# Gated linear attention: the decayed queries times the state on quarters of the array, right behind the level products, into two PSUM banks; the next queries' transposes in another bank

## The chip, the cores and the metric

The kernel is one inference step of one layer of a hybrid decoder. It runs on one core of a Trainium2 chip. The metric is device time in microseconds (us) from one launch to its end; of several executions the median is given. The engines of the core are TensorE (PE in the profile; its weight loads are listed apart as PEld), VectorE (DVE), ScalarE (ACT), GpSimd (POOL) and SyncE (SP), which here issues the DMAs. Matmuls read SBUF and write PSUM, whose eight banks hold 512 float32 numbers for each of 128 partitions.

## The reference

The layer has two groups of heads behind one input projection (sliding-window attention and gated linear attention), an output projection, and a squared-ReLU MLP. The change is in the gated linear attention of the 2048 prompt tokens: 4 heads, keys and queries of 64, values of 128. Per head there is a state S of 64 x 128, which starts at zero. Cut to what matters:

```python
b = jnp.cumsum(log_a, axis=2)                      # inside a chunk
attn = einsum('bnthk,bntshk->bnhts', qc, exp(causal(b_t - b_s)) * kc)
o_intra = einsum('bnhts,bnshv->bnthv', attn, vc)
q_dec = qc * exp(b)                                # the decayed queries
def step(S, xs):
    o = einsum('bthk,bhkv->bthv', qd, S)           # decayed queries times the state
    S = ab[..., None] * S + einsum('bthk,bthv->bhkv', kd, vv)
    return S, o
o = o_intra + o_inter                              # then RMSNorm, gate, output projection
```

The outputs are the tokens after the layer, the last 128 keys and values, and the states.

## The kernel before

The kernel goes through the tokens in stages: input projection of the attention columns with windowed attention, input projection of the linear-attention columns (tiles named gproj) with the gated linear attention in between, output projection (out), and the two MLP matrices (u... and dn). The change lies in the second of these, at about 330 to 690 us.

**Chunks.** The 2048 tokens are 16 chunks of 128, index i. `gla(i, ...)` is a generator that does one chunk. At each `yield n` the loop that drives it issues n matmuls of other work on TensorE, the "fill": the projection of later chunks (gproj, 128 x 384 each) and near the end the output projection. The numbers are in `G_FILL = (34, 14, 16, 8, 20)`. TensorE executes in the order in which the calls stand (its wrapper, line 142, chains every instruction to the one before), so this list sets how much other work stands between two steps of a chunk. The order on VectorE and ScalarE is made by a scheduler, within the dependencies; where two instructions must not change places the code says so.

**Steps of a chunk.** (1) `qk_T`: four transposes (tile gqk) bring keys and queries to 128 partitions, which hold two heads of 64. VectorE copies the keys (kt); ScalarE copies the queries to `qz[rows, r]`, r = 0 or 1 for the upper or lower 64 partitions, the other half being zero. (2) After 34 fills the norm and gate of the chunk before are finished (`finish_out`: squares on ScalarE, line 1180, tile og on VectorE, line 1189) and transposed (ogT); then z, the gate of the next chunk, is projected into bank "d". (3) VectorE and ScalarE make the weighted keys and queries of 7 levels (XK, XQ), which treat the triangle of a chunk block by block, and kd, the keys decayed to the chunk's end. (4) The level products: tiles gl and gh in two banks of kind "c", then ds, the new part of the state, in bank "d". The level products and ds have 128 rows and 64 columns of the array each, and write to partitions 0 to 63 and 64 to 127 in turn. (5) VectorE multiplies qz by the decay to get qd, of 128 x 2 x 2 x 128, half of it zero (line 1269). (6) VectorE puts the level products into AH under masks (line 1163), VectorE and ScalarE copy them to AT, the triangle transposed (lines 1273 to 1275, the names `put` and `done`); VectorE then makes the next state (line 1280, which reads ds). (7) After 20 fills, tile o in bank "e": per head first qd times the state So, then AT times the values gv, summed in PSUM; each is a float32 product on the whole array, 128 x 128 by 128 x 128.

The PSUM banks "d" and "e" are there once, "a", "b" and "c" twice; a tile takes over a bank when all readers of the tile before are done. In the profile the two passes of a float32 product are two MATMUL rows, each with a weight load.

Of the kernel before, what the change touches and what calls it, by code (L numbers as in the profile page):

```python
# [16 lines left out]
ALU = mybir.AluOpType  # L17
# [4 lines left out]
P = 128  # L22
# [19 lines left out]
NL = len(LEVELS)  # L42
# [85 lines left out]
def f32(ap):  # L128
    return ap.bitcast(F32)
# [23 lines left out]
def hybrid_step_kernel(ctx: ExitStack, tc: tile.TileContext, I, O):  # L153
    nc = tc.nc
# [18 lines left out]
    te, ac, dv = (InOrder(tc, engine) for engine in (nc.tensor, nc.scalar, nc.vector))  # L173
# [4 lines left out]
    def bank(shape, kind, name):  # L178

        return ps.tile(shape, F32, tag=kind, name=name, bufs=1 if kind in "de" else 2)  # L180
# [240 lines left out]
    half_of = slice(HD), slice(HD, P)  # L421
# [606 lines left out]
    def places(name, shape, n=1, kind=F32):  # L1028
        return cycle([sp.tile(shape, kind, name=f"{name}{u}") for u in range(n)])

    S = [sp.tile([P, 2, P], F32, name=f"S{u}") for u in range(2)]
    glrT = [sp.tile([P, P], F32R, name=f"glrT{u}") for u in range(3)]
    AT = sp.tile([P, 4, P], F32, name="AT")
# [3 lines left out]
    XK = sp.tile([P, NL, 2, P], F32, name="XK")  # L1037
    XQ = sp.tile([P, NL, 2, 2, P // 2], F32, name="XQ")
    sgs, prs = places("sg", [P, 512]), places("pr", [P, 256])
    qds = places("qd", [P, 2, 2, P])  # L1040
    decs = places("dec", [P, NL + 1, 2, P])
    befores, afters = places("before", [P, 2, P]), places("after", [P, 2, P])
    kts = places("kt", [P, 2, P], 2)
    qz = sp.tile([P, 2, 2, P], F32, name="qz")
# [58 lines left out]
    def qk_T(i, gp, n, kind="d"):  # L1103

        pt = bank([P, 2, 2, n], kind, f"gqk_{i}")
        for g in range(2):
            for a in range(2):
                src = gp[:n, (1 - a) * 256 + g * P : (1 - a) * 256 + (g + 1) * P]
                te.transpose(pt[:, g, a, :], src, ident[:n, :n])
        kt, q = (next(kts), qz) if n == P else (s_kt, s_qz)  # L1110
        nc.vector.tensor_copy(kt, pt[:, :, 0, :])
        for r, rr in enumerate(half_of):
            nc.scalar.activation(q[rr, r], pt[rr, :, 1, :], AF.Copy, scale=0.125)
        return kt
# [60 lines left out]
    def finish_out(i, og_src, sg, n, kind):  # L1175

        ssq = sp.tile([P, 4], F32, tag="ossq", name=f"ossq_{i}", bufs=2)
        junk = sp.tile([P, P], mybir.dt.bfloat16, tag="ojunk", name=f"ojunk_{i}", bufs=1)
        for h in range(4):
            nc.scalar.activation(junk[:n], og_src(h), AF.Square, accum_out=ssq[:n, h : h + 1])  # L1180
        rs = sp.tile([P, 4], F32, tag="ors", name=f"ors_{i}", bufs=2)
        rsqrt_mean(sp, rs[:n], ssq[:n], n, P, 4)
        if i == NB:
            yield 44, True
            yield 44, True
        og = next(ogs) if i < NB else gp_s[:, :512].rearrange("p (h d) -> p h d", h=4)
        for h in range(4):
            with tc.issue_after(put[0].ins) if i == NB else nullcontext():
                nc.vector.scalar_tensor_tensor(
                    og[:n, h, :], og_src(h), rs[:n, h : h + 1], sg[:n, h * P : (h + 1) * P],  # L1190
                    op0=ALU.mult, op1=ALU.mult,
                )
        for _ in range(S_WAIT[0] if i == NB else 1):
            yield 44, True
        pt = bank([P, 4, P], kind, f"ogT_{i}")
        for h in range(4):
            te.transpose(pt[:, h, :n], og[:n, h, :], ident[:n, :n])
        if i == NB - 1:
            hi, lo = late_mix
            nc.vector.tensor_copy(hi, pt)  # L1200
            nc.vector.tensor_tensor(lo, pt, f32(hi), op=ALU.subtract)
        else:
            mo = next(mos)
            nc.scalar.activation(mo[:, :, :n], pt[:, :, :n], AF.Copy)
            nc.sync.dma_start(mix_d[i][:, 4:8, :], mo[:, :, :n])

    def decayed(i):

        before, after = next(befores), next(afters)
        yield from decays(i, P, before, "d" if i else "b")  # L1210
        nc.gpsimd.memset(after, 0.0)
        pre[i] = before, after

    def gla(i, gp, og=iter(())):

        assert {(i, 0), (i, 1)} <= projected
        before, after = pre.pop(i)
        next(og, None)  # L1220
        kt = qk_T(i, gp, P)
        dec = next(decs)
        following = decayed(i + 1) if i < NB - 1 else iter(())
        yield G_FILL[0] + 3 * (i == 1) if i else G_FIRST_FILL, True
        deque(og, 0)
        put_diagonal(i, AH, gp, P)
        for l, b in enumerate(LEVELS):
            if l < (4 if i == 2 else NL - 1) or i == 0:
                level_sums(before, after, dec, l, b)
            else:  # L1230
                with tc.issue_after(put[0].ins):
                    level_sums(before, after, dec, l, b)
            if l == NL - 1:
                kd = next(kds)
                pair = i // 2 + 1 if i % 2 == 0 and i < NB - 2 else 0
                turned = keys_decayed(after, kt, next(kdTs), P, "e", kd, pair)
                nc.scalar.activation(dec[:, NL], before, AF.Exp, scale=1.0 / 16)
            weighted(XK, XQ, dec, kt, qz, l, b)
        next(turned)
        deque(following, 0)  # L1240
        yield G_FILL[1] - 3 * (i == 1), True
        assert {(i, c) for c in range(4)} <= projected
        sg = gate(i, gp, P)
        yield G_FILL[2], True
        deque(turned, 0)
        yield G_FILL[3], True
        low = bank([P, 4, 4, P // 4], "c", f"gl_{i}")
        high = bank([P, 512], "c", f"gh_{i}")
        mid = high[:, :256].rearrange("p (l h q) -> p l h q", l=2, h=4)
        far = high[:, 256:384].rearrange("p (r q) -> p r q", r=2)  # L1250
        levels = [*(low[:, l] for l in range(4)), *(mid[:, l] for l in range(2))]
        for l, gm in enumerate(levels):
            for g in range(2):
                keys = XK[:, l, g] if l else kt[:, g]
                for u, uu in enumerate(half_of):
                    te.matmul(
                        gm[uu, 2 * g : 2 * g + 2], keys[:, uu], XQ[:, l, :, g, u * 32 : u * 32 + 32], start=True, stop=True
                    )
        for g in range(2):
            te.matmul(far[half_of[g]], XK[:, NL - 1, g, :HD], XQ[:, NL - 1, :, g], start=True, stop=True)  # L1260
        gv = gp[:, 512:1024]
        ds = bank([P, 2, P], "d", f"ds_{i}")
        for h in range(4):
            te.matmul(
                ds[half_of[h % 2], h // 2], kd[:, h * HD : (h + 1) * HD], gv[:, h * P : (h + 1) * P],
                start=True, stop=True,
            )
        qd = next(qds)
        nc.vector.tensor_tensor(qd, qz, dec[:, NL].unsqueeze(1).to_broadcast([P, 2, 2, P]), op=ALU.mult)
        for l, gm in enumerate(levels):  # L1270
            put_level(AH, gm, msk[:, l], LEVELS[l])
        for g in range(2):
            nc.scalar.activation(AT[:HD, 2 * g : 2 * g + 2, HD:], far[half_of[g]], AF.Copy)
        put[:] = [nc.vector.tensor_copy(AT[half_of[1], :, half_of[1]], AH[half_of[1]])]
        done = nc.scalar.activation(AT[half_of[0], :, half_of[0]], AH[half_of[0]], AF.Copy)
        put.append(done)
        So, Sn = S[i % 2], S[(i + 1) % 2]
        with tc.issue_after(put[0].ins):
            for g in range(2):
                nc.vector.scalar_tensor_tensor(  # L1280
                    Sn[:, g], So[:, g], dec[:, NL, g, P - 1 : P], ds[:, g], op0=ALU.mult, op1=ALU.add
                )
        yield G_FILL[4], True
        o_ = bank([P, 4, P], "e", f"o_{i}")
        for h in range(4):
            if i > 0:
                te.matmul(o_[:, h, :], qd[:, h % 2, h // 2], So[:, h // 2], start=True, stop=False)
            te.matmul(o_[:, h, :], AT[:, h, :], gv[:, h * P : (h + 1) * P], start=i == 0, stop=True)
        with tc.issue_after(done.ins):
            next(wo_parts, None)  # L1290
        ogs_of[i] = og = finish_out(i, lambda h: o_[:, h, :], sg, P, "e")
        if i == NB - 1:
            yield from og
            for g in range(2):
                for r in range(2):
                    nc.sync.dma_start(O["gla_prompt"][0, 0, 2 * g + r], Sn[half_of[r], g])
# [229 lines left out]
    wo, pre, ogs_of, mixes, late_mix, g_mix, put, placing, x1_first = {}, {}, {}, {}, [], [], [], [], []  # L1526
# [887 lines left out]
```

## Time and profile before

| | |
|---|---|
| median of 3 runs | 2162.13 us (2161.69 to 2163.29) |
| the profiled execution | 2162.71 us, its span 2160.9 us |
| TensorE busy | 2149.6 us, 99% of the span |
| VectorE, ScalarE, GpSimd busy | 71%, 57%, 12% |
| mean granted TensorE clock | 0.999 |
| MATMUL rows o<-S,qd in the trace | 120 (15 chunks of 4 products of 2 passes) |

A row of the time line has the start in us, the length in us, engine, line, operation, output tile <- input tiles, the rows and columns of the array (64\*64 means that one quarter of it is used), the shape that is streamed, and the count of instructions merged. Matmuls overlap, so that what one costs is the distance to the next start and not its length. Idle time in brackets says which engine ended it; "issue" is idle time for which the trace has no releaser.

### The profile page before, as it was taken

The numbers are of one execution on the slowest core, as the hardware profiler recorded it, in microseconds if no ns is written. First come the engines' busy times: TensorE is split into PE (matmuls) and PEld (weight loads), VectorE is DVE, ScalarE is ACT, GpSimd is POOL, SyncE is SP. The second block draws the span as 40 slices with busy tenths as digits, with TensorE's granted clock in tenths as the row PEclk, the third lists the DMA queues.
The fourth block names the chain that finished last, engine by engine and source line by source line (L and its number), as shares of the span: only waits on it lengthen the run. The fifth ranks groups of instructions, "written<-read, shape, count | busy, mean of one in ns | idle before, by whom it ended". The sixth has DMA issues, their size and how long they took to land.

```text
span 2160.9 us, 34240 instructions
## 1 busy us (share of the span) xinstructions
PE 2149.6 (99%) x11799; PEld 1864.0 (86%) x11799; DVE 1529.1 (71%) x3203; ACT 1221.6 (57%) x2625; POOL 258.5 (12%) x417
## 2 busy tenths in 40 slices
PE   9999999999999999999999999999999999999998
PEld 9999999999998888888888888888888888888887
DVE  7999868777775766988888545547766666555566
ACT  7999867566664444655555544445454445444454
POOL 4676511111111100000000000000000000000000
PEclk9999999999999999999999999999999999999999
DMA  7444341234338566777785777668544443766685
GB/s 242 154 147 148 99 117 40 71 106 135 136 126 270 199 216 220 245 269 274 256 279 208 269 247 223 208 199 274 183 171 155 157 150 126 257 203 195 195 267 181
DMA packets 241322, 411.54 MB, mean 190 GB/s; under 512 B 24876, under 2 KB 143132, under 8 KB 237036
## 3 DMA queue, kind: packets, MB, share of 16 engines
q1 hardware_dynamic: 240988, 409.08, 57.1%
q8 instruction: 93, 1.52, 0.3%
q14 instruction: 81, 0.66, 0.1%
q10 hardware_dynamic: 160, 0.27, 0.0%
HBM read 265.82 MB, written 143.99 MB: 190 GB/s over the span
## 4 chain that ended last, share of the span: by engine, by line
PE 93%; DVE 2%; ACT 2%; DMA 1%; issue 1%; POOL 0%; SPq 0%; DVEq 0%; POOLq 0%; ACTq 0%
PE dn L142 27%; PE gproj L142 13%; PE uc L142 8%; PE uX L142 8%; PE out L1419 7%; PE proj L142 6%; PE ue L142 4%; PE ud L142 4%; PE ub L142 4%; PE dsam L142 1%; PE sam L142 1%; PE o L142 1%; PE sc L142 1%; PE pT L142 1%; PE av L142 1%; PE out L142 1%
## 5 line engine op out<-in xcount | busy, mean ns | idle before, releaser
L142 PE MATMUL dn<-o1t,o0s 128*128 128x512 f32 x892 | 347.9, 390 | 0.8 <-DVE o1t L229 0.8
L142 PE MATMUL dn<-o0t,o1s 128*128 128x512 f32 x892 | 347.7, 390 | 0.0
L142 PE MATMUL dn<-o0t,o0s 128*128 128x512 f32 x892 | 347.4, 389 | 0.3 <-DVE f L2075 0.3
L229 DVE TENSOR_TENSOR o1s<-rs,o0s 128x512 fp32r<-128x512 f32 x224 | 154.6, 691 | 220.8 <-ACT o0s L228 218.5
L228 ACT ACTIVATE o0s<-rs 128x512 fp32r<-128x512 f32 x224 | 141.1, 631 | 291.9 <-PE dn L142 261.6
L142 PE MATMUL gproj<-wg,gxh 128*128 128x384 f32 x1024 | 273.2, 342 | 0.0
L142 PEld LDWEIGHTS dn<-o1t,o0s 128*128 128x128 f32 x892 | 167.4, 188 | 37.3 <-DVE o1t L229 1.7
L142 PEld LDWEIGHTS dn<-o0t,o0s 128*128 128x128 f32 x892 | 167.5, 188 | 36.8 <-DVE f L2075 0.7
L142 PEld LDWEIGHTS dn<-o0t,o1s 128*128 128x128 f32 x892 | 167.4, 188 | 35.2
L142 ACT ACTIVATE st<-st 128x512 f32<-128x512 f32 x224 | 141.1, 630 | 100.2 <-DVE st L142 95.1
L142 PEld LDWEIGHTS gproj<-wg,gxh 128*128 128x128 f32 x1024 | 184.2, 189 | 3.5 <-issue 3.1
L142 PE MATMUL uc<-H,s 128*128 128x512 f32 x768 | 186.5, 391 | 0.1
L142 PE MATMUL gproj<-wg,gxl 128*128 128x384 f32 x576 | 185.9, 340 | 0.0
L142 PE MATMUL uX<-H,w 128*128 128x512 f32 x768 | 185.2, 390 | 0.0
L142 PEld LDWEIGHTS uX<-H,w 128*128 128x128 f32 x768 | 144.0, 188 | 30.3
L142 PEld LDWEIGHTS uc<-H,s 128*128 128x128 f32 x768 | 143.0, 188 | 30.6 <-ACT st L142 0.3
L1419 PE MATMUL out<-wo,mt 128*128 128x512 f32 x680 | 158.6, 392 | 0.0
L229 DVE TENSOR_TENSOR o1t<-rt,o0t 128x512 fp32r<-128x512 f32 x223 | 152.7, 685 | 5.3 <-ACT o0t L228 3.7
L218 POOL TENSOR_TENSOR frs<-rs_v,half 128x1 f32<-128x1 f32 (+1 forms) x13 | 11.5, 891 | 1198.6 <-DVE rs_v L216 1198.6
L1419 PEld LDWEIGHTS out<-wo,mt 128*128 128x128 f32 x680 | 126.5, 188 | 26.1
L228 ACT ACTIVATE o0t<-rt 128x512 fp32r<-128x512 f32 x223 | 137.7, 618 | 7.5 <-DMA rt<-t_d 4.8
L142 DVE TENSOR_TENSOR st<-st 128x512 f32<-128x512 f32 x160 | 110.7, 692 | 30.1 <-ACT st L142 25.8
(429 smaller groups left out, 4307.2 us busy)
## 6 DMA issues: line engine op xcount, KB each, us to landing
s_d<-st SPq DMA_DIRECT2D x32, 1792.0 KB, 8.9
rs<-s_d SPq DMA_DIRECT2D x224, 256.0 KB, 3.0
raw<-in_w_up SPq DMA_DIRECT2D x64, 512.0 KB, 4.6
rt<-t_d SPq DMA_DIRECT2D x128, 256.0 KB, 3.9
rt<-in_w_down SPq DMA_DIRECT2D x96, 256.0 KB, 2.9
t<-in_w_down SPq DMA_DIRECT2D x64, 256.0 KB, 3.7
t_d<-t SPq DMA_DIRECT2D x32, 512.0 KB, 5.1
h_d<-ht SPq DMA_DIRECT2D x8, 1280.0 KB, 7.6
```

The source lines that it names most:

```text
L142: ins = call(*a, **k)
L218: return nc.gpsimd.tensor_tensor(out, v[:n], e, op=ALU.pow)
L228: nc.scalar.activation(hi, src, AF.Copy)
L229: return vector.tensor_tensor(lo, src, f32(hi), op=ALU.subtract)
L1419: te.matmul(banks[c], x, w[:, c * 512 : (c + 1) * 512], start=k + u == 0, stop=k == KT - 1 and u == len(products) - 1,)
```

## The change

In step 5 the decayed queries are made without the zero half, in two VectorE instructions of 64 partitions x 256 (qd is now 128 x 2 x 128), ahead of the first fill of step 3 to 4 instead of behind the level products.

The products of qd and the state leave step 7. They stand right behind ds in step 4, and instead of 4 products on the whole array there are 8 of 64 rows x 64 columns: r is the half of the rows (one head), u the half of the queries, hence of the output partitions, g the pair of heads. The results of r = 0 go to bank "e", those of r = 1 to the right half of the bank "d" whose left half holds ds. The products of AT and the values stay where they were and add to the two banks; `finish_out` reads both.

The transposes of the next chunk's keys and queries (gqk) go to a bank of kind "c" instead of "d", which is now occupied until og is made.

```diff
-    qds = places("qd", [P, 2, 2, P])
+    qds = places("qd", [P, 2, P])
...
-        kt = qk_T(i, gp, P)
+        kt = qk_T(i, gp, P, "c")
...
         next(turned)
+        qd = next(qds)
+        for r, rr in enumerate(half_of):
+            nc.vector.tensor_tensor(qd[rr], qz[rr, r], dec[rr, NL], op=ALU.mult)
         deque(following, 0)
         yield G_FILL[1] - 3 * (i == 1), True
...
-        ds = bank([P, 2, P], "d", f"ds_{i}")
+        fourth = bank([P, 4, P], "d", f"ds_{i}")
+        ds = fourth[:, :2]
...
-        qd = next(qds)
-        nc.vector.tensor_tensor(qd, qz, dec[:, NL].unsqueeze(1).to_broadcast([P, 2, 2, P]), op=ALU.mult)
+        So, Sn = S[i % 2], S[(i + 1) % 2]
+        o_ = bank([P, 2, P], "e", f"o_{i}"), fourth[:, 2:]
+        for g in range(2):
+            for u, uu in enumerate(half_of):
+                for r, rr in enumerate(half_of):
+                    if i > 0:
+                        te.matmul(
+                            o_[r][uu, g], qd[rr, g, uu], So[rr, g], start=g == 0, stop=False, skip_group_check=True
+                        )
...
-        o_ = bank([P, 4, P], "e", f"o_{i}")
         for h in range(4):
-            if i > 0:
-                te.matmul(o_[:, h, :], qd[:, h % 2, h // 2], So[:, h // 2], start=True, stop=False)
-            te.matmul(o_[:, h, :], AT[:, h, :], gv[:, h * P : (h + 1) * P], start=i == 0, stop=True)
+            te.matmul(
+                o_[h % 2][:, h // 2], AT[:, h, :], gv[:, h * P : (h + 1) * P], start=i == 0, stop=True, skip_group_check=True
+            )
...
-        ogs_of[i] = og = finish_out(i, lambda h: o_[:, h, :], sg, P, "e")
+        ogs_of[i] = og = finish_out(i, lambda h: o_[h % 2][:, h // 2], sg, P, "e")
```

How the instructions stand: TensorE in one even chunk in the middle of the stage, from the level products to the next queries' transposes, before (S is the state, gp the values and keys, the fill gproj is left out).

```order
L142 MATMUL gh_7494<-XQ,XK 64x128 x2
L142 MATMUL ds_7521<-gp_7093,kd_4983 64x128 [waits DVE_49,Activation_49]
L142 MATMUL ds_7521<-gp_7093,kd_4983 64x128 x3
...
L142 MATMUL o_7559<-S_4976,qd_4991 128x128 [waits PE_49,Activation_49]
L142 MATMUL o_7559<-gp_7093,AT 128x128 [waits DVE_49,Activation_49]
L142 MATMUL o_7559<-S_4976,qd_4991 128x128
L142 MATMUL o_7559<-gp_7093,AT 128x128
...
L142 MATMUL gqk_7591<-ident,gp_7361 128x128 [waits DVE_49,PE_49]
```

The same place in the changed kernel; the new products that write to bank "d" are listed under the name ds.

```order
L142 MATMUL gh_7532<-XQ,XK 64x128 x2
L142 MATMUL ds_7559<-gp_7124,kd_4983 64x128 [waits DVE_49,Activation_49]
L142 MATMUL ds_7559<-gp_7124,kd_4983 64x128 x3
L142 MATMUL o_7564<-S_4976,qd_4991 64x128 [waits PE_49,Activation_49]
L142 MATMUL ds_7559<-S_4976,qd_4991 64x128
...
L142 MATMUL o_7564<-gp_7124,AT 128x128 [waits DVE_49,Activation_49]
L142 MATMUL ds_7559<-gp_7124,AT 128x128 [waits DVE_49]
...
L142 MATMUL gqk_7632<-ident,gp_7397 128x128 [waits PE_49]
```

Eight small products now stand directly behind ds, in turns into the two banks; the four of the whole array are gone from between the AT products; the second AT product has a wait for VectorE of its own, and gqk no longer waits for VectorE.

VectorE in one chunk, from the last weighted keys to the next chunk's gate, before:

```order
L1132 TENSOR_TENSOR XQ<-dec_4992,qz 128x256
L1137 TENSOR_TENSOR kdT_5000<-kdT_5000,kt_4995 128x256
L1095 SCALAR_TENSOR_TENSOR sg_4989<-gp_7093,sg_4989 128x512 [waits DVE_49,Activation_49]
L1269 TENSOR_TENSOR qd_4991<-qz,dec_4992 128x512
L1086 SCALAR_TENSOR_TENSOR before_4993<-z_7430,zt_4998 128x256 [waits PE_49,Activation_49]
```

and now:

```order
L1132 TENSOR_TENSOR XQ<-dec_4992,qz 128x256
L1137 TENSOR_TENSOR kdT_5000<-kdT_5000,kt_4996 128x256
L1242 TENSOR_TENSOR qd_4991<-qz,dec_4992 64x256 x2
L1095 SCALAR_TENSOR_TENSOR sg_4989<-gp_6831,sg_4989 128x512 [waits DVE_49,Activation_49]
L1086 SCALAR_TENSOR_TENSOR before_4993<-z_7199,zt_4999 128x256 [waits PE_49,Activation_49]
```

The scheduler had already put qd this early; it moves by one place, ahead of the gate's product, and is two instructions.

More of the change, by code (lines that the diff above doesn't have):

```diff
@@ L1276, in gla @@
         put.append(done)
-        So, Sn = S[i % 2], S[(i + 1) % 2]
         with tc.issue_after(put[0].ins):
```

## The prediction

> **What bounds the kernel now.** I read the page first: which engine is full, and whose chain ended last.
>
> ```profile
> PE 2149.6 (99%) x11799; PEld 1864.0 (86%) x11799; DVE 1529.1 (71%) x3203; ACT 1221.6 (57%) x2625; POOL 258.5 (12%) x417
> PE 93%; DVE 2%; ACT 2%; DMA 1%; issue 1%; POOL 0%; SPq 0%; DVEq 0%; POOLq 0%; ACTq 0%
> ```
>
> TensorE is the bound overall. Whether it is in the stage that changes is read from the busy times by window: the whole stage with what follows, and single chunks, from one chunk's first level product to the next's.
>
> ```profile
> 330.00:690.00 360.00, 359.98 (x2975) 342.37 (x2974) 272.28 (x819) 224.64 (x668) 61.05 (x62) 1.00 0.36 121
> 690.00:1200.00 510.00, 509.93 (x2444) 426.26 (x2443) 392.06 (x612) 267.20 (x466) 19.20 (x33) 1.00 0.73 244
> 539.16:560.75 21.59, 21.59 (x183) 1.00 0.38 135
> 560.75:582.38 21.63, 21.63 (x182) 1.00 0.40 135
> ```
>
> PE is busy in 359.98 of 360 us, VectorE in 272. "Busy" can hide a stretched matmul, so I looked at the waits of the weight loads in that stretch too:
>
> ```profile
> PEld gl L142 <- issue: 4.0, 15, 0.4
> PEld o L142 <- ACT AT L1275: 0.2, 1, 0.2
> ```
>
> Only one wait of the step that changes is there, 0.2 us once; the first row is 15 entries into the level products and returns below. So the stage lasts as long as its matmuls take, and the following stage runs TensorE just as full (509.93 of 510): time saved on TensorE here comes off the end.
>
> **What is removed.** One chunk's o, before:
>
> ```profile
> 544.94 0.38 PE L142 MATMUL o<-S,qd 128*128 128x128 f32 x2
> 545.16 0.39 PE L142 MATMUL o<-gp,AT 128*128 128x128 f32 x2
> 545.38 0.39 PE L142 MATMUL o<-S,qd 128*128 128x128 f32 x2
> ...
> 546.72 0.49 PE L142 MATMUL gqk<-ident,gp 128*128 128x128 f32 x3
> ```
>
> Eight products in 546.72 - 544.94 = 1.78 us, 0.22 each (0.111 per pass). Four go: 0.89 us per chunk, in the 15 chunks that have a state. The four AT products stay.
>
> **What is added.** Eight products, sixteen passes, of 128 columns streamed on quarters of the array. No row has just that, so I take the nearest. First the level products and ds, which use half the columns:
>
> ```profile
> 538.89 0.34 PE L142 MATMUL gproj<-wg,gxh 128*128 128x384 f32 x1
> 539.16 0.45 PE L142 MATMUL gl<-XQ,kt 128*64 128x64 f32 x8
> ...
> 540.83 0.61 PE L142 MATMUL ds<-gp,kd 128*64 128x128 f32 x8
> 541.36 0.45 PE L142 MATMUL gproj<-wg,gxh 128*128 128x384 f32 x1
> 541.64 0.34 PE L142 MATMUL gproj<-wg,gxl 128*128 128x384 f32 x1
> ```
>
> A gproj normally starts 0.17 after the one before (the pair in the next fence); into gl it takes 539.16 - 538.89 = 0.27, so 0.10 is lost on entering; the "issue" row above is these 15 entries as the weight loads see them (4.0 / 15 = 0.27). ds has 8 passes in 0.53; if as much is lost on leaving, 0.43 remain: two passes at a time, 0.11 per pair, the column halves running together. Then the two places that use fewer rows:
>
> ```profile
> 396.34 0.33 PE L142 MATMUL gproj<-wg,gxh 128*128 128x384 f32 x1
> 396.51 0.33 PE L142 MATMUL gproj<-wg,gxl 128*128 128x384 f32 x1
> 396.77 0.65 PE L142 MATMUL sds<-gp_s,s_kx 64*64 64x128 f32 x8
> 397.35 0.62 PE L142 MATMUL gproj<-wg,gxh 128*128 128x384 f32 x2
> ```
>
> ```profile
> 288.01 0.38 PE L142 MATMUL spt<-ident,ss 128*128 128x128 f32 x2
> 288.32 0.44 PE L142 MATMUL ssc<-kc,qs 64*32 64x128 f32 x8
> 288.56 0.31 PE L142 MATMUL ssc<-kns,qs 64*32 64x64 f32 x8
> ```
>
> sds is the shape of the new products, but all of it on one half of the rows: 0.58 us for 8 passes, of which 0.10 is leaving and about 0.04 the first loads: again pairs at 0.11. ssc has four column groups: 8 passes of 128 columns in 0.24 us, that is four at a time, 0.11 per set and 0.02 more for the first. So independent parts of the array do run together here; what no row shows is the two halves of the rows at once. The Trainium skill, "TensorE: Matmul & The Clock Gate", section "Part 3: Packing small matmuls — row/col tiling", has measured speedups for tiles packed in rows and columns at once; no run here shows that yet.
>
> I take four at a time: 4 sets x 0.11 = 0.44, plus 0.03 for the first loads. Between ds (128 rows) and the new products (64 rows) the array changes its division, and I charge the 0.10 of the other entries: spt to ssc shows it too (288.32 - 288.01 = 0.31 for two passes of 0.11, 0.09 over). Leaving costs the same from sds (397.35) as from ds, so nothing is added there. Block: 0.57 us. Low end 0.44 (no drain, ds and the new products alike to the array), high end 0.44 + 0.03 + 0.20 = 0.67 (drain paid as on entering and on leaving). The Trainium skill, "TensorEngine Tiling (Array Packing)", section "Key Properties", has it that a change of tiling mode, not of tile, drains the array; by that 0.57 holds and not 0.44. The entries above agree with it, but between two divided modes no row stands.
>
> Saved per chunk: 0.89 - 0.57 = **0.32**; over 15 chunks 4.8 us (3.3 at 0.67, 6.8 at 0.44).
>
> **Waits.** AT must be ready when TensorE comes to it. The tightest two chunks:
>
> ```profile
> 566.14 0.60 DVE L1280 SCALAR_TENSOR_TENSOR S<-S,dec,ds 128x128 f32<-128x128 f32 x2
> 566.34 0.40 ACT L1275 ACTIVATE AT<-AH 64x256 f32<-64x256 f32 x1
> 566.53 0.38 PE L142 MATMUL o<-S,qd 128*128 128x128 f32 x2
> ```
>
> ```profile
> 625.46 0.45 PE L142 MATMUL gl<-XQ,kt 128*64 128x64 f32 x8
> 631.19 0.40 ACT L1275 ACTIVATE AT<-AH 64x256 f32<-64x256 f32 x1
> 631.24 0.38 PE L142 MATMUL o<-S,qd 128*128 128x128 f32 x2
> 631.65 0.49 PE L142 MATMUL o<-gp,AT 128*128 128x128 f32 x2
> ```
>
> In the second, AT ends at 631.59 and the first AT product starts 0.41 after the first qd product instead of 0.22: 0.19 is lost. In the changed kernel the block stands ahead of the 20 fills, so TensorE gets to AT at 631.24 + 0.57 = 631.81 by the same clock, 0.22 after AT is there: that wait goes, **0.2 us** in all. The new second wait, of the AT product into bank "d" for the state update that reads ds, ends at 566.74 in the first fence; TensorE comes to it at 566.53 + 0.57 + 0.22 = 567.32. Behind both would stand the next chunk's gqk and all fill. The new products themselves wait for bank "e", in even chunks for the copy of glrT:
>
> ```profile
> 518.76 0.27 ACT L1145 ACTIVATE glrT<-kdT 128x128 fp32r<-128x128 f32 x1
> 519.34 0.61 PE L142 MATMUL ds<-gp,kd 128*64 128x128 f32 x8
> ```
>
> It ends 0.3 us before ds starts. Bank "d" is now held until og is made, and z wants it next; but z stands behind ogT, which needs og anyway. gqk in "c" needs a bank whose reader was the masked copy, done before AT. These edits cost nothing, as long as og stays ahead of ogT: 549.93 + 1.13 = 551.06 against 553.07.
>
> ```profile
> 549.93 1.13 DVE L1189 SCALAR_TENSOR_TENSOR og<-o,ors,sg 128x128 f32<-128x128 f32 x4 [0.46 <-POOL ors L218]
> 553.07 0.60 PE L142 MATMUL ogT<-ident,og 128*128 128x128 f32 x4
> 554.12 0.69 DVE L1269 TENSOR_TENSOR qd<-qz,dec 128x512 f32<-128x512 f32 x1
> 556.57 0.42 DVE L1086 SCALAR_TENSOR_TENSOR before<-z,zt 128x256 f32<-128x256 f32 x1 [1.76 <-ACT zt L980]
> ```
>
> **VectorE.** qd was 0.69; now two instructions of 64 x 256. A product of 256 columns of this kind takes 0.42 (the row at 556.57), whatever its partitions, so 0.84 at most, 0.15 more per chunk. VectorE idles 1.76 us right behind it, waiting for ScalarE; that covers it. Without that cover the masked copies would come 0.15 later, still inside the 0.22 of the tightest chunk.
>
> **Sum.** 4.8 + 0.2 = 5.0 us off the profiled execution's 2162.71 us: 2157.7. That execution is 0.6 above the median, so against 2162.13 I predict **2157.1 us**. One thing moves single executions without the change:
>
> ```profile
> 376.70:380.15 3.45, 3.45 (x36) 0.51 0.34 89
> ```
>
> Here the granted clock was 0.51 for one stretch of 3.4 us, behind a stretch of very small products of the sample tokens: some 1.7 us lost. The three runs differ by 1.6. Whether a later run has this stretch I can't tell; it widens the range by about 1 us.
>
> **Rivals.**
>
> *No drain* between ds and the new products: block 0.44, saved 6.8 + 0.2 = 7.0, 2155.1 us. For it: the columns are divided in two before and after, only the rows change. Against: every change of division in the trace costs about 0.10. Chance 0.12.
>
> *Loads in the open or a double drain:* if the weight loads of a quarter can't run under the products of the same rows, each of the four sets waits for its load. The nearest price is the pair of gl passes of 64 columns, which bounds a load of 64 columns: (540.14 - 539.44) / 12 = 0.058.
>
> ```profile
> 539.44 0.87 PE L142 MATMUL gl<-XQ,XK 128*64 128x64 f32 x24
> 540.14 0.86 PE L142 MATMUL gh<-XQ,XK 128*64 128x64 f32 x20
> ```
>
> Three more loads are 0.17, the block 0.74, saved 2.3 + 0.2: 2159.6 us. The Trainium skill, "TensorE: Matmul & The Clock Gate", section "Part 3: Packing small matmuls — row/col tiling", says that loads overlap with running products only if the row group differs, which is this rival. Against it: sds has all its products on one row group, and 0.11 per pair leaves no room for a load of its own. Chance 0.10.
>
> *The halves of the rows don't run together:* eight pairs instead of four sets, 8 x 0.11 + 0.13 = 1.01 us against 0.89 removed. **Slower** by 0.12 x 15 = 1.8, less the 0.2: 2163.7 us. It decides from a set time of 0.19 up (4 x 0.19 + 0.13 = 0.89). For it: no row shows two halves of the rows at once. Against: four column groups run together at the full rate, and the two halves write to different banks. Chance 0.09.
>
> *AT becomes the bound:* in a chunk like the one at 566 TensorE reaches AT at 566.53 + 0.57 = 567.10, 0.36 us after ScalarE and VectorE are done. If their new order delays the masked copies by more than that in most chunks, the next 0.32 takes the gain (2162) and each further 0.1 costs 1.5 us. Against: the order of VectorE around the copies stays. Chance 0.04.
>
> **Chances.** The forecast has 0.65, and its own range is 2156.0 to 2158.6 (a block from 0.52 to 0.62, and the odd half-clock stretch). A difference of 0.2%, 4.3 us, is about what a measurement of this kernel can tell from none: faster means below 2157.8. Of the forecast's 0.65 some 0.48 lies there, with the 0.12 of no drain 0.60. Slower, above 2166.5, has 0.03, from AT as the bound and a second failure. The rest, 0.37, is the same. The range 2154.7 to 2160.0 takes in all but the last two rivals.
>
> **What would show it.** In the trace of after: sixteen rows of 64\*64 behind ds, with about 0.55 to 0.6 us from their first start to the next gproj less 0.10 for leaving; if they take 1.0, the row halves do not run together. The o rows shrink to four products of 0.22. The period of the chunk at 539 falls from 21.59 to about 21.27. No wait of o for VectorE or ScalarE. The prediction is wrong if the rows of 64\*64 come in pairs 0.11 apart, if "issue" in front of them is well over 0.1, or if a stage behind this one turns out to wait for a DMA that did not move.

## The result: 0.15% slower, and the profile after

The median of 21 runs is 2165.21 us (2162.84 to 2167.74); the kernel before, run beside it, has 2161.90 (2159.75 to 2164.71, 21 runs). The ratio is 1.0015, with a 95% interval of 1.0010 to 1.0021: 3.3 us slower, where 5.0 us faster was forecast. On TensorE itself the change did what it was to do. The page of the changed kernel, total busy times and the chain that ended last:

```profile
PE 2147.0 (99%) x11919; PEld 1856.3 (86%) x11919; DVE 1537.2 (71%) x3219; ACT 1220.7 (56%) x2625; POOL 259.6 (12%) x417
PE 88%; DVE 6%; ACT 4%; issue 1%; DMA 1%; POOL 0%; DVEq 0%; ACTq 0%; SPq 0%
```

TensorE is busy for 2.6 us less than before, but VectorE and ScalarE, 2% each of the chain before, now hold 10% of it together. The busy times of the stage, and of one chunk in its middle (columns: span; then PE, PEld, VectorE, ScalarE and GpSimd busy; clock; DMA share; GB/s), show where:

```profile
330.00:690.00 360.00, 353.02 (x3047) 331.50 (x3042) 276.75 (x826) 222.73 (x662) 61.49 (x62) 1.00 0.36 118
537.92:559.90 21.98, 21.51 (x191) 20.60 (x190) 17.58 (x51) 14.46 (x42) 3.91 (x4) 1.00 0.39 133
```

TensorE was busy for 359.98 of these 360 us and now is for 353.02; the next stage, 690 to 1200 us, is as full as it was (510.00 of 510). The waits of the weight loads in the same stretch (engine, what waited, for what: us in all, times, the longest):

```profile
PEld ds L142 <- ACT kd L1143: 9.2, 9, 1.6
PEld o L142 <- issue: 2.5, 14, 0.3
```

The first row is new. In nine chunks ds waits for kd, the copy of the decayed keys on ScalarE, 9.2 us in all. The second is the entering of the new block, 14 times 0.18. Here is that block, in the chunk of the second window above (TensorE's time line):

```profile
540.23 0.66 PE L142 MATMUL ds<-gp,kd 128*64 128x128 f32 x8 [0.47 <-ACT kd L1143]
540.82 0.32 PE L142 MATMUL o<-S,qd 64*64 64x128 f32 x1
540.82 0.32 PE L142 MATMUL ds<-S,qd 64*64 64x128 f32 x1
540.83 0.32 PE L142 MATMUL o<-S,qd 64*64 64x128 f32 x1
540.84 0.32 PE L142 MATMUL ds<-S,qd 64*64 64x128 f32 x1
540.98 0.27 PE L142 MATMUL o<-S,qd 64*64 64x128 f32 x1
...
541.09 0.27 PE L142 MATMUL o<-S,qd 64*64 64x128 f32 x1
...
541.19 0.27 PE L142 MATMUL o<-S,qd 64*64 64x128 f32 x1
...
541.41 0.44 PE L142 MATMUL gproj<-wg,gxh 128*128 128x384 f32 x1
...
544.98 0.38 PE L142 MATMUL o<-gp,AT 128*128 128x128 f32 x2
...
545.87 0.60 PE L142 MATMUL gqk<-ident,gp 128*128 128x128 f32 x4
```

Sixteen passes come in four sets of four, both halves of the rows and of the columns at once: the sets start at 540.82, 540.98, 541.09 and 541.19, and the next gproj at 541.41. That is 0.59 us, of which 0.10 is leaving. The products of AT alone take 545.87 - 544.98 = 0.89. So the saving is there, and more than its size is lost ahead of ds.

**Why kd is late.** VectorE in one chunk of the kernel before, from the copy of the keys kt to qd; its queries' transposes gqk started at 503.64:

```profile
503.64 0.60 PE L142 MATMUL gqk<-ident,gp 128*128 128x128 f32 x4
504.28 0.42 DVE L1111 COPY kt<-gqk 128x256 f32<-128x256 f32 x1 [0.38 <-PE gqk L142]
504.74 0.90 DVE L1130 TENSOR_TENSOR XK<-dec,kt 128x128 f32<-128x128 f32 x4
505.56 0.17 DVE L216 TENSOR_SCALAR rs_v<-ossq 128x4 f32<-128x4 f32 x1
...
506.85 1.13 DVE L1189 SCALAR_TENSOR_TENSOR og<-o,ors,sg 128x128 f32<-128x128 f32 x4 [0.46 <-POOL ors L218]
...
510.11 0.42 DVE L1137 TENSOR_TENSOR kdT<-kdT,kt 128x256 f32<-128x256 f32 x1
510.53 0.69 DVE L1095 SCALAR_TENSOR_TENSOR sg<-gp,sg 128x512 f32<-128x512 f32 x1
511.14 0.68 DVE L1269 TENSOR_TENSOR qd<-qz,dec 128x512 f32<-128x512 f32 x1
```

The same chunk of the changed kernel:

```profile
502.15 0.60 PE L142 MATMUL gqk<-ident,gp 128*128 128x128 f32 x4
502.79 0.42 DVE L1111 COPY kt<-gqk 128x256 f32<-128x256 f32 x1
503.25 0.49 DVE L1130 TENSOR_TENSOR XK<-dec,kt 128x128 f32<-128x128 f32 x2
504.29 0.17 DVE L216 TENSOR_SCALAR rs_v<-ossq 128x4 f32<-128x4 f32 x1 [0.55 <-ACT ojunk L1180]
504.37 0.51 DVE L1130 TENSOR_TENSOR XK<-dec,kt 128x128 f32<-128x128 f32 x2
505.58 0.35 DVE L1189 SCALAR_TENSOR_TENSOR og<-o,ors,sg 128x128 f32<-128x128 f32 x1 [0.70 <-POOL ors L218]
...
509.37 0.42 DVE L1137 TENSOR_TENSOR kdT<-kdT,kt 128x256 f32<-128x256 f32 x1
509.71 0.84 DVE L1242 TENSOR_TENSOR qd<-qz,dec 64x256 f32<-64x256 f32 x2
510.58 0.69 DVE L1095 SCALAR_TENSOR_TENSOR sg<-gp,sg 128x512 f32<-128x512 f32 x1
```

Two things differ on VectorE. First, the norm's small step rs_v and og of the chunk before stand behind two and four of the products XK, where they stood behind four, and then behind one XK and one XQ more (the scheduler put them there; this order appears in ten of the twelve chunks from the fifth on). Neither is ready: VectorE idles 0.55 us for ScalarE's squares and 0.70 for GpSimd, where it had idled 0.46. So kdT ends 509.79 - 502.15 = 7.64 us behind gqk and not 510.53 - 503.64 = 6.89: 0.75 later. Second, qd now stands ahead of the gate's product sg, which starts 0.79 behind the end of kdT (510.58 - 509.79) where it had started right at it: sg ends 9.12 us behind gqk and not 7.58.

ScalarE's last step of the gate (L1096) waits for sg, and steps of zt, made from z of the next chunk, stand behind it: three before, two now, since the first (L977) has changed places with it. Before, and after:

```profile
511.26 0.64 ACT L1096 ACTIVATE sg<-sg 128x512 f32<-128x512 f32 x1 [0.76 <-DVE sg L1095]
512.28 0.38 ACT L977 ACTIVATE zt<-z 128x256 f32<-128x256 f32 x1
513.13 0.42 ACT L980 ACTIVATE zt<-zt 128x256 f32<-128x256 f32 x1
518.50 0.36 ACT L1143 ACTIVATE kd<-kdT 128x256 f32<-128x256 f32 x1
```

```profile
509.62 0.38 ACT L977 ACTIVATE zt<-z 128x256 f32<-128x256 f32 x1
511.31 0.63 ACT L1096 ACTIVATE sg<-sg 128x512 f32<-128x512 f32 x1 [1.31 <-DVE sg L1095]
512.28 0.42 ACT L980 ACTIVATE zt<-zt 128x256 f32<-128x256 f32 x1
517.92 0.37 ACT L1143 ACTIVATE kd<-kdT 128x256 f32<-128x256 f32 x1
```

So zt ends 9.91 us behind gqk before and 10.55 after, 0.64 later, while sg is 1.54 later. sg has a second follower: behind L1096 GpSimd multiplies the gate twice (L1098, L1100), and in the changed kernel the second of these meets the first sums of the levels on VectorE:

```profile
513.46 1.56 POOL L1100 TENSOR_TENSOR sg<-sg,ggla 128x512 f32<-128x512 f32 x1
513.78 1.38 DVE L1157 TENSOR_TENSOR before<-before 128x128 f32<-128x128 f32 x1
```

This sum takes 1.38 us. In the traces of the ten kernels of this document 137 such sums between 400 and 650 us start inside one of GpSimd's two multiplications. Each ends 0.14 to 0.15 us behind it and takes up to 1.39 us; every other such sum takes at most 0.30. VectorE is held there until GpSimd is done. It happens 18 times in each of the four kernels with qd ahead of the gate's product, and 10 or 11 times in each of the six others.

Behind zt VectorE and ScalarE take turns through the levels of the next chunk (before, after, dec), and kd stands in ScalarE's queue behind most of these exponentials. It ends 15.22 us behind gqk before (518.86 - 503.64) and 16.14 after (518.29 - 502.15); ds comes at 519.34 - 503.64 = 15.70 when nothing holds it. kd had half a microsecond to spare in this chunk, 0.23 in the tightest of the stage's middle. And the lateness is passed on: the next gqk stands behind this ds on TensorE, and its kt, og and kdT behind that. The middle chunks (the eight that start between 470 and 630 us) go from one to the next in 22.24 us on average, where it was 21.58 before.

This is a reading of two traces, in which two delays are mixed; the experiments separate them.

### The profile page after: what moved, and what is told of

Its sections match the earlier page's. It is cut to its first block, busy times and chain, and to the rows that moved or that the text cites. A ratio compares the mean times of both kernels' runs of the same rounds, so it can differ in the third digit from the quotient of the medians.

```text
span 2164.4 us, 34502 instructions
## 1 busy us (share of the span) xinstructions
PE 2147.0 (99%) x11919; PEld 1856.3 (86%) x11919; DVE 1537.2 (71%) x3219; ACT 1220.7 (56%) x2625; POOL 259.6 (12%) x417
## 3 DMA queue, kind: packets, MB, share of 16 engines
q8 instruction: 94, 1.54, 0.3%
## 4 chain that ended last, share of the span: by engine, by line
PE 88%; DVE 6%; ACT 4%; issue 1%; DMA 1%; POOL 0%; DVEq 0%; ACTq 0%; SPq 0%
PE dn L142 27%; PE uc L142 8%; PE uX L142 8%; PE out L1428 7%; PE gproj L142 7%; PE proj L142 6%; PE ud L142 4%; PE ue L142 4%; PE ub L142 4%; PE sam L142 2%; PE dsam L142 1%; PE sc L142 1%; PE pT L142 1%; PE av L142 1%; PE out L142 1%
```

## The experiments

All times are medians of 11 runs, against 33 of the kernel before on the same chip beside them: 2161.74 us for the first four kernels, 2161.56 for the other four. The waits given are those of the weight loads between 330 and 690 us.

### qd behind the gate

```diff
-        qd = next(qds)                # ahead of the first 14 fills
-        for r, rr in enumerate(half_of):
-            nc.vector.tensor_tensor(qd[rr], qz[rr, r], dec[rr, NL], op=ALU.mult)
...
         sg = gate(i, gp, P)
+        qd = next(qds)
+        for r, rr in enumerate(half_of):
+            nc.vector.tensor_tensor(qd[rr], qz[rr, r], dec[rr, NL], op=ALU.mult)
```

> The changed kernel with its two qd instructions on VectorE moved from ahead of the gate's product (sg, L1095) to directly behind it. Nothing is left out. Theory 1 (qd's place alone makes the copy kd late): the gate's product ends some 0.8 us earlier, ScalarE's exponential for it no longer holds up the logarithms of zt, kd comes back ahead of ds, ds waits for kd in sum under 1 us in the stretch of the middle chunks (9.0 us in the changed kernel), and the time is about 2157.2, what the prediction gave. Theory 2 (the next queries come 0.6 us sooner behind AT than VectorE can take them, so its whole chain and kd stay late): only part comes back, the wait falls to 4 to 6 us and the time is about 2160 to 2161. Rival (the bank of the next queries): nothing changes, about 2165.

Measured: 2160.46 us, ratio 0.9993 (0.9984 to 1.0001). One move on VectorE gives back 4.7 us of the changed kernel's 2165.21. In the trace:

```profile
PEld ds L142 <- ACT kd L1143: 3.3, 6, 1.1
```

So qd's place is a cause, and not the only one: theory 1, which expected 2157.2, falls. rs_v and og stand as early as in the changed kernel here, and kdT is as late (qd stands behind the gate's product in 12 of the 15 chunks, as in the kernel before). Nor is it by the logarithms that kd comes back. In the same chunk, whose gqk starts at 500.64:

```profile
510.79 0.42 ACT L980 ACTIVATE zt<-zt 128x256 f32<-128x256 f32 x1
511.07 1.30 POOL L1100 TENSOR_TENSOR sg<-sg,ggla 128x512 f32<-128x512 f32 x1
511.70 0.82 DVE L1156 TENSOR_TENSOR after<-after,before 128x128 f32<-128x128 f32 x1
515.86 0.37 ACT L1143 ACTIVATE kd<-kdT 128x256 f32<-128x256 f32 x1
```

zt ends 10.6 us behind gqk, as in the changed kernel. But GpSimd's second multiplication ends at 11.73 and not at 12.87, VectorE's sum is held for less, and kd ends at 15.59 and not at 16.14. Over eight middle chunks zt differs by 0.03 us, GpSimd's end by 0.79 and kd by 0.63. That qd's place costs the time is shown by the two kernels; the way through GpSimd is read from their traces, since no run moves GpSimd's work alone.

### The bank of the next queries alone

```diff
-        kt = qk_T(i, gp, P)
+        kt = qk_T(i, gp, P, "c")
```

> The kernel before with one thing of the change: the next chunk's queries gqk go to bank c. Nothing is left out. Theories 1 and 2: no difference, about 2162 (gqk's bank was not waited for). Rival (the bank): about 3 us slower, 2165, with a wait of gqk or of the products that use bank c in the trace.

Measured: 2161.33 us, ratio 0.9996 (0.9987 to 1.0005), no wait of gqk or gl that was not there before. The bank by itself is not the cause: the rival's 3 us lie outside the interval, which goes from 2.8 us faster to 1.1 us slower.

### qd early in the kernel before

```diff
         next(turned)
+        qd = next(qds)
+        nc.vector.tensor_tensor(qd, qz, dec[:, NL].unsqueeze(1).to_broadcast([P, 2, 2, P]), op=ALU.mult)
         deque(following, 0)
...
-        qd = next(qds)                # behind the level products
-        nc.vector.tensor_tensor(qd, qz, dec[:, NL].unsqueeze(1).to_broadcast([P, 2, 2, P]), op=ALU.mult)
```

> The kernel before with one thing of the change: its qd (still one instruction of 128x512, 0.69 us) is moved on VectorE ahead of the gate's product, to where the changed kernel has its two. Nothing is left out. Theory 1: the gate's product and kd come about 0.7 us later; kd had about 0.25 us to spare ahead of ds, so ds waits about 0.4 us in some 11 chunks: 4 to 5 us slower than before, about 2166.5, and TensorE shows a wait of ds for kd. Theory 2: the same wait but less of it, since TensorE isn't faster here: 1 to 4 us slower. Rival (the bank): no difference, 2162.

Measured: 2163.44 us, ratio 1.0006 (0.9997 to 1.0015), which can't be told from no change by its interval. The trace has the wait, and small:

```profile
PEld ds L142 <- ACT kd L1143: 1.5, 4, 0.5
```

The same order that costs 4.7 us in the changed kernel costs 1.7 here by the medians, and 3.2 at most by the interval. Theory 1 expected 4 to 5 and is wrong again; theory 2's 1 to 4 fits. rs_v and og stand late here, kd comes only 0.36 later on average over the middle chunks, and what it had to spare in TensorE's longer chunk covers most of that.

### The transposes for kd six fills earlier

```diff
-G_FILL = (34, 14, 16, 8, 20)
+G_FILL = (34, 14, 10, 14, 20)
```

> The changed kernel with the transposes for kd put six fill products (about 1 us of TensorE) earlier, ahead of six of the fills that had stood before them; qd stays ahead of the gate's product. Nothing is left out. Theories 1 and 2: if the copy kd is what ends last, it comes earlier with its source and ds waits less: 2157 to 2160. If kd is only held up in ScalarE's queue, behind exponentials for which VectorE comes late, and not by its source, ds waits as before: about 2165. Rival (the bank): no difference, 2165.

Measured: 2164.89 us, ratio 1.0013 (1.0004 to 1.0022): nothing gained. Neither of the two mechanisms that I had put down for this case is what the trace shows:

```profile
PEld o L142 <- ACT AT L1286: 7.3, 10, 1.3
PEld ds L142 <- ACT kd L1143: 1.4, 4, 0.4
```

kd was moved, since it stands earlier in ScalarE's queue now, and ds no longer waits much. But the AT products wait 7.3 us instead. VectorE and ScalarE are late with a whole chunk, not with one copy, and whichever of their results TensorE asks for first shows the wait. The middle chunks take 22.18 us each, almost as in the changed kernel (22.24).

That left two explanations: that the loop through VectorE and ScalarE is really longer than TensorE's shortened chunk, or that its order makes it so. The next kernels pin rs_v and og behind the products that they had stood behind.

### Both orders set back

On top of the kernel with qd behind the gate. The first five products XK of chunks 4 to 15 are written ahead of the steps of the norm, which are told to stand behind the fourth and the fifth of them (cut to these lines):

```diff
-        rsqrt_mean(sp, rs[:n], ssq[:n], n, P, 4)
+        with tc.issue_after(ahead[3].ins) if ahead else nullcontext():
+            rsqrt_mean(sp, rs[:n], ssq[:n], n, P, 4)
...
-            with tc.issue_after(put[0].ins) if i == NB else nullcontext():
+            with tc.issue_after(put[0].ins) if i == NB else tc.issue_after(ahead[4].ins) if ahead else nullcontext():
...
-        next(og, None)
+        if not PIN(i):
+            next(og, None)
         kt = qk_T(i, gp, P, "c")
         dec = next(decs)
+        if PIN(i):
+            for l, b in enumerate(LEVELS[:6]):
+                with tc.issue_after(put[0].ins) if l >= 4 and i == 2 else nullcontext():
+                    level_sums(before, after, dec, l, b)
+                if l:
+                    ahead.append(nc.vector.tensor_tensor(pairs(XK[:, l], b, 0), pairs(dec[:, l], b, 0), pairs(kt, b, 0), op=ALU.mult))
+            next(og, None)
```

In the trace rs_v stands behind five XK in most chunks, one more than in the kernel before, and og behind five XK and one XQ, as there.

> The changed kernel with two orders on VectorE set back as they were before, in chunks 4 to 15: qd behind the gate's product (as in e1), and the norm's small step (rs_v) and the multiplication og behind five products of the weighted keys, where the changed kernel has them behind two and four. Nothing is left out. Theory A (VectorE's order alone, in these two places, makes kd late): VectorE idles some 0.7 us less between kt and kdT per chunk, the sum of the waits of ds for kd falls from 3.3 us in e1 to under 1, and the time is 2157 to 2158, what the prediction gave. Theory B (the loop of VectorE and ScalarE is as long as the shortened chunk on TensorE, whatever the order): ds or the AT products still wait 3 us or more, and the time stays at about 2160.

Measured: 2156.95 us, ratio 0.9981 (0.9972 to 0.9990): 4.6 us under the kernel before beside it. For the change 2157.1 had been forecast, 5.0 under. The wait of ds and the busy times of the stage:

```profile
PEld ds L143 <- ACT kd L1146: 1.4, 4, 0.6
```

```profile
330.00:690.00 360.00, 359.45 (x3098) 337.86 (x3093) 277.83 (x836) 226.84 (x672) 63.64 (x64) 1.00 0.38 125
```

TensorE is full again, with VectorE no less busy than in the changed kernel (277.83 against 276.75): order, not work, had kept TensorE waiting. Theory B falls. The wait that is left is 1.4 us and not under 1.

### Only rs_v and og set back

The same pins on the changed kernel, with qd left ahead of the gate.

> The changed kernel with only the second of the two orders set back: rs_v and og behind the weighted keys; qd stays ahead of the gate's product. Nothing is left out. Theory A: the two delays add, 0.7 to 0.8 us each, and this one goes: the wait of ds for kd falls from 9 us to 2 to 4, the time is about 2160 to 2161. Theory B: the wait hardly falls, about 2163 to 2165.

Measured: 2161.63 us, ratio 1.0005 (0.9996 to 1.0014); it gives back 3.6 us of the changed kernel's 2165.21.

```profile
PEld ds L143 <- ACT kd L1146: 6.2, 8, 1.1
```

The wait fell less than theory A expected, to 6.2 and not to 2 to 4 us, and the time is 0.6 above its 2160 to 2161. With this run the four combinations are complete:

| | rs_v, og early (as changed) | rs_v, og behind the keys | difference |
|---|---|---|---|
| qd ahead of the gate (as changed) | 2165.21 | 2161.63 | 3.6 |
| qd behind the gate | 2160.46 | 2156.95 | 3.5 |
| difference | 4.7 | 4.7 | |

The two delays add, here within 0.1 us, which is less than these medians can be trusted to. The kernel before had 2161.90 us beside the changed kernel, 2161.74 beside the one with qd alone set back and 2161.56 beside the other two; taken from it each time, the differences are 4.6 and 4.7 for qd and 3.2 and 3.3 for the norm. Together the delays cost 7.9 us so, 8.3 by the medians alone.

### Both set back, and kd two fills earlier

```diff
-G_FILL = (34, 14, 16, 8, 20)
+G_FILL = (34, 14, 14, 10, 20)
```

> As e5, and the transposes for kd two fill products (0.35 us of TensorE) earlier, so that kd can end earlier ahead of ds. Nothing is left out. Theory A: with the loop no longer late this gives the rest: no wait of ds for kd, 2156.5 to 2157.5. Theory B: the wait moves on to the AT products, as in the kernel with six fewer, and the time is about 2160.

Measured: 2156.29 us, ratio 0.9978 (0.9969 to 0.9987). This is the fastest kernel of the study by its median, 5.3 us under the one before it; its difference from the kernel with both set back, 0.7 us, lies inside the intervals. One wait for kd of 0.2 us is left in the stage, where the changed kernel had 9.2 us:

```profile
330.00:690.00 360.00, 360.00 (x3123) 338.58 (x3123) 278.85 (x841) 228.62 (x677) 63.02 (x63) 1.00 0.38 125
```

Its middle chunks take 21.25 us each on average, 0.33 less than the 21.58 before. The forecast from the rows was 0.32.

### The quarter products in another order

On top of the kernel with both orders set back: the four calls on the upper 64 rows first, then the four on the lower.

```diff
-        for g in range(2):
-            for u, uu in enumerate(half_of):
-                for r, rr in enumerate(half_of):
+        for r, rr in enumerate(half_of):
+            for g in range(2):
+                for u, uu in enumerate(half_of):
```

So TensorE's list reads, in each chunk,

```
MATMUL o<-S,qd 64x128 x4
MATMUL ds<-S,qd 64x128 x4
```

> As e5, with the eight quarter products in another order: the four of the upper 64 rows of the array first, then the four of the lower 64. Nothing is left out. If only neighbours in the order run together, on different rows and columns, sixteen passes now come in eight pairs of 0.11 us and not in four sets: the block takes 0.44 us more, over 15 chunks 6.6 us more than e5, about 2164. If TensorE finds the four quarters whatever the order, no difference.

Measured: 2156.41 us, ratio 0.9980 (0.9971 to 0.9989), no difference from 2156.95. TensorE's time line in one chunk:

```profile
536.45 0.33 PE L143 MATMUL o<-S,qd 64*64 64x128 f32 x2
536.48 0.33 PE L143 MATMUL ds<-S,qd 64*64 64x128 f32 x2
536.61 0.28 PE L143 MATMUL o<-S,qd 64*64 64x128 f32 x2
536.64 0.28 PE L143 MATMUL ds<-S,qd 64*64 64x128 f32 x2
```

The first two passes of ds start 0.03 us behind the first two of o. The other six passes of o stand ahead of them in the list and start later. The quarters find each other across the list, at least over these four calls.

## Why the prediction was wrong

Forecast were 2157.1 us and faster; measured were 2165.21, above the whole range of 2154.7 to 2160.0.

- **What bounds the kernel.** Right for the kernel before, and taken as right for the one after. The prediction looked for waits, found one of 0.2 us in the step that changes, and did not ask how near others were to being waits. The copy kd had 0.23 us to spare ahead of ds in the tightest of the middle chunks, and the prediction does not name it.
- **Removed, 0.89 us per chunk.** Right: the four AT products left take 0.89.
- **The new block, 0.57 us.** Right. In the last kernel but one, whose stage is full, ds and the block take 1.13 us from the first pass of ds to the next gproj (559.10 to 560.23); ds alone took 0.54 before (519.34 to 519.88). So the block takes 0.59: four sets, the first 0.16 and the others 0.11, and 0.10 for the change of division ahead of it. Of the rivals, *no drain* (0.44), *loads in the open* (0.74) and *the halves of the rows don't run together* (1.01) are excluded by these rows. The rule from the Trainium skill, "TensorEngine Tiling (Array Packing)", section "Key Properties", that a change of mode drains the array, agrees with the trace: 0.10 us. The one in "TensorE: Matmul & The Clock Gate", section "Part 3: Packing small matmuls — row/col tiling", that loads overlap only if the row group differs, does not: every set after the first reloads the same rows, at 0.11 us per set.
- **VectorE: the step that failed.** The prediction put it so: "VectorE idles 1.76 us right behind it, waiting for ScalarE; that covers it." The idle time covers VectorE's own next step, which waits for zt: with qd ahead of the gate's product or behind it, zt ends 10.66 and 10.69 us behind gqk on average over eight middle chunks. It covers nothing else that waits for sg. qd had moved ahead of sg, as the order of VectorE ahead of the prediction shows; the price was taken as the 0.15 us by which qd grew, and sg came later by 0.79. So did GpSimd's multiplications of the gate, which then held VectorE's sums of the levels, and kd came 0.63 later (16.56 us behind gqk against 15.93 over the same chunks). It costs 4.7 us (2165.21 against 2160.46, and 2161.63 against 2156.95). The cost of qd's place is shown by these two pairs; the way through GpSimd is read from the traces.
- **The order that the prediction left out.** rs_v and og moved by two places on VectorE, and the prediction reads VectorE's new order only around qd. It costs 3.5 us: the waits behind kt grow (0.55 and 0.70 us in the chunk shown, where it was 0.46), because the steps that were moved forward wait for ScalarE and GpSimd, and VectorE does not pass on to what stands behind them.
- **The rival "AT becomes the bound"** was the nearest to what happened. It had 0.04, since "the order of VectorE around the copies stays". There it stays; the order 10 us earlier does not. In the kernel with kd six fills earlier it came true, 7.3 us of waits for AT.
- **Edits costed at nothing.** The bank of gqk shows no cost, as said. Nor does the longer hold of banks "d" and "e": no wait for them shows.

The sum itself was good: with both orders set back 4.6 of the 5.0 us come, and 5.3 with kd two fills earlier as well. Wrong was that the other engines would keep up with a TensorE that had become faster.

## What to carry to other kernels

Where one engine is full, look at how near each of its inputs is to being late, not only at the waits that there are; a change that shortens its loop by 0.3 us uses up a margin of 0.23. Idle time of an engine behind a moved instruction covers it for that engine's next step alone: follow what the instruction has overtaken to every engine that waits for it, and ask what each will then run into (here GpSimd, and VectorE again). And where a scheduler makes the order, an edit on one engine may move instructions on another that it does not mention: read the new order of every engine for the whole loop, ask of each step that moved forward whether it is ready there, and pin what must not move.

## What was not expected of the hardware

A sum of 128x128 on VectorE that takes 0.29 us takes up to 1.39 when it starts while GpSimd multiplies the gate, and ends 0.14 to 0.15 us behind GpSimd's instruction, in each of the 137 cases counted above. A GpSimd step that nothing on TensorE waits for soon can so delay one that TensorE does wait for.

TensorE does not need the products for its quarters in turns: with all four calls of one half of the rows ahead of the four of the other, it starts both halves within 0.03 us, and the sets of four follow each other at the same 0.11 us. The Trainium skill, "TensorE: Matmul & The Clock Gate", section "Part 3: Packing small matmuls — row/col tiling", says that matmuls start and end strictly in the order of the program; these rows start in another, between different quarters.
